# All sixteen gates ahead of the branches, and head pairs multiplied q first, then k, in a hybrid decoder step on one core

## The chip, the cores and the metric

The kernel runs on one core of one Trainium2 chip, in float32. The metric is the device time of one execution in microseconds (us); runs of a kernel on this one core agree within about 0.1%. Engines are named as in the profile: PE is TensorE (matrix products; PEld is its weight load), DVE is VectorE, ACT is ScalarE, POOL is GpSimd, SP is SyncE, which here issues most of the DMAs. SBUF is the on-chip memory, PSUM holds what TensorE writes.

## The reference

One layer (`DEPTH = 1`) of a hybrid decoder, for a prompt of 512 tokens and 8 single-token samples, 1024 wide. Both go through the same weights, so the kernel lays them side by side as 520 columns.

```
mod = silu(c) @ w_mod + b_mod                  # six parts: sh1, sc1, g1, sh2, sc2, g2
h   = rmsnorm(x) * (1 + sc1) + sh1
qa, fa, ia, oga, xb, yb, ga, gb = split(h @ w_in)      # eight parts of 1024
# branch A, HGRN2, 8 heads of 128: per token S = diag(f) S + k (x) v, o = S^T q
q = silu(qa); f = lb + (1 - lb) * sigmoid(fa); k = (1 - lb) * sigmoid(-fa)
o_a = rmsnorm(hgrn2(q, k, ia, log f)) * silu(oga)
# branch B, RG-LRU: causal conv of width 4, block-diagonal gates, a linear scan over time
o_b = rglru(conv(xb)) * gelu(yb)
merged = sigmoid(ga) * (o_a @ w_branch_a) + sigmoid(gb) * (o_b @ w_branch_b)
x = x + g1 * (merged @ w_out)
x = x + g2 * (relu(h2 @ w_ff1)^2 @ w_ff2),  h2 = rmsnorm(x) * (1 + sc2) + sh2
y = rmsnorm(x)
```

The final states of both recurrences are outputs too. The "gates" of this document are the two products with `ga` and `gb`, eight tiles of 128 rows each: sixteen in all. They depend on `h` alone; the products with `w_branch_a` and `w_branch_b` depend on the recurrences' results.

## The kernel before

**Products.** Everything is kept transposed, features on partitions, tokens along the row. A product (`gemm`, line 151 through `products`) makes 128 output rows for all 520 columns: 8 blocks of the sum, two column halves of 260, and three matmuls for each, because each float32 operand is split in a high and a low part that TensorE takes fast (`hi*hi + hi*lo + lo*hi`), 48 matmuls in all. It writes one of two PSUM tiles `mm`. A weight tile of 512 KB is loaded by SP into one of four slots `wst` (lines 101 and 103), rounded by ScalarE to `whi` (line 112) and subtracted by VectorE to `wlo` (line 115). `weights` sorts all tiles of the program in a fixed order: a tile is split two products ahead (`AHEAD`) and loaded three entries ahead (`LOADS`). Rows of w_mod (`ROWS`) go through the same slots and are used from there unsplit.

**Stages.** `begin` makes the modulation and `h`. Then come eight heads (`head`), each with four products (f, q, output gate, v), and between them the RG-LRU tiles (`rg_x`, `rg_y`). After each odd head, `heads_prompt` does the recurrence of the last two heads for the prompt. Then come the eight b gates, the eight products with w_branch_b, and eight times an a gate and the product with w_branch_a (`merge`); then w_out, and the MLP, which fills the second half of the time. Sixteen `mod` steps (two row tiles of w_mod, 16 small matmuls, line 413) are strewn among gates and branches by fixed rules (`mod_step`); they accumulate in PSUM pool `ppt`, which has one buffer, `pt`, and which the heads use too.

**heads_prompt.** A chunk of 128 tokens is treated by doubling: at level b (1, 2, 4, ... 64) TensorE takes the products of k of each block with q of the block after it (lines 664, 669, 673), then VectorE multiplies the decay of a block into the second blocks' q and the first blocks' k (line 681), VectorE or ScalarE picks the level's entries out (lines 688 and 691), and VectorE multiplies neighbouring decays into those of the next level (line 698). `X` holds, for each head, q times its decay (row 0), k (row 1) and q (row 2); four such tiles serve the eight heads in turn. `self.together()` raises the priority of what stands in it by 400.

**Order.** The program is a list of steps; a scheduler goes by priority (the program's order, unless raised) and its own estimate of readiness, and writes one fixed order for each engine. So an instruction may be ahead of an earlier step's, but at run time each engine keeps to that order.

**The hand-over.** After b gate number `TAIL` two steps stand: `end_recurrences` (the samples' norm, line 754 on) and `begin_tail`, which closes the pools of the heads, opens `misc`, `abb`, `tail` and `ab` in their memory and calls `load_branches`: 16 DMAs on POOL (lines 883 and 887) bring the recurrences' results back from DRAM, and ScalarE and VectorE split them (lines 205 and 206) to `a` (branch b's input) and `b` (branch a's). `reuse_waits="tile"` means that a tile in reused memory waits only for the old tiles it lies on. b gates use the eight slots `ma`, a gates two at a time the slots `t` of `tail`. The last work of a pair of heads is a row norm (lines 738 to 743), a transpose (747), the output multiplication (749), a store by SP (750), and for the samples line 632 and 634.

Of the kernel before, what the change touches and what calls it, by code (L numbers as in the profile page):

```python
# [6 lines left out]
F32 = mybir.dt.float32  # L7
# [4 lines left out]
OP = mybir.AluOpType  # L12
# [4 lines left out]
L = 512  # L17
NB = 8
T = L + NB
HALF = T // 2  # L20
KO = D // 128
# [3 lines left out]
DFF = 4 * D  # L25
EPS = 1e-6
AHEAD = 2
TAIL = 3
URGENT = 200
TOGETHER = 400  # L30
NWM = 8
# [45 lines left out]
class Kernel:  # L77
# [458 lines left out]
    def head_f(self, h, ps):  # L536

        nc = self.nc
        f = self.slot(self.ma, "ma")
        X = self.X[h % 4]  # L540
        k = X[:, 1]
        with self.urgent():
            self.sigmoid(self.two(f), ps)
            self.sigmoid(self.two(k), ps, scale=-1.0)
        nc.vector.tensor_scalar(f, f, self.lb1[:, h:h + 1], self.lbf[:, h:h + 1], OP.mult, OP.add)
        nc.vector.tensor_scalar(k, k, self.lb1[:, h:h + 1], None, OP.mult)
        return f, X

# [86 lines left out]

    def heads_prompt(self, hs):
        nc = self.nc
        two = [self.opened[h] for h in hs]
        tbs = [x[0][:, :L] for x in two]
        Xs = [x[1] for x in two]  # L640
        Ts = [self.hg.tile([128, 508], F32, name="tb", bufs=2) for _ in hs]
        to = 0
        a32 = self.hg.tile([128, 2, NC, 32], F32, name="a32", bufs=1)
        at = self.at

        def view(t, first_q, first_k, step, n, b):

            return bass.AP(tensor=t.tensor, offset=t.offset + first_q,
                           ap=[t.ap[0], [T + first_k - first_q, 2], [step, n], [1, b]])

        heads = lambda m, *shape: m[:, None].to_broadcast([128, 2, *shape])
        b = 1
        while b < C:
            n = L // (2 * b)
            p = self.pps.tile([128, 512], F32, name="ps")
            with self.together():
                for e, X in enumerate(Xs):
                    Q, K = X[:, 0], X[:, 1]
                    for c in range(NC):
                        if b == 1:  # L660
                            for j in range(4):
                                s, o = c * C + 32 * j, 256 * e + 64 * c
                                o = p[32 * j:32 * j + 32, o:o + 64].rearrange("p (x t) -> p x t", x=2)
                                nc.tensor.matmul(o, K[:, s:s + 32], X[:, 0::2, s:s + 32], start=True, stop=True)
                        elif b <= 32:
                            for j in range(0, 128, 32 if b < 32 else 64):
                                s, o = c * C + j, 128 * e + 32 * c
                                d = s if b < 32 else s + 32
                                nc.tensor.matmul(p[j:j + 32, o:o + 32], K[:, s:s + 32], Q[:, d:d + 32], start=True,
                                                 stop=True)  # L670
                        else:
                            s, o = c * C, 256 * e + 64 * c
                            nc.tensor.matmul(p[:64, o:o + 64], K[:, s:s + 64], Q[:, s + 64:s + 128], start=True,
                                             stop=True)
                if b == 64:
                    po = self.heads_sample(hs)
            for X, tb in zip(Xs, tbs):
                half = view(X, b, 0, 2 * b, n, b)
                fac = bass.AP(tensor=tb.tensor, offset=tb.offset, ap=[tb.ap[0], [1, 2], [2, n], [0, b]])
                with self.together():  # L680
                    nc.vector.tensor_tensor(half, half, fac, OP.mult)  # L681
            if b == 1:
                first = p.rearrange("p (e c x t) -> p e c x t", e=2, c=NC, x=2)
                nc.vector.tensor_tensor(a32, first[:, :, :, 1], heads(self.mdiag, NC, 32), OP.mult)
                p = first[:, :, :, 0]
            if b <= 16:
                p = p if b == 1 else p[:, :256].rearrange("p (e c t) -> p e c t", e=2, c=NC)
                nc.vector.copy_predicated(a32, heads(self.masks[b], NC, 32), p)
            elif b == 32:
                for j in (0, 64):  # L690
                    nc.scalar.copy(at[j:j + 32, :, :, j + 32:j + 64],
                                   p[j:j + 32, :256].rearrange("p (e c t) -> p e c t", e=2, c=NC))
            else:
                nc.scalar.copy(at[:64, :, :, 64:], p[:64].rearrange("p (e c t) -> p e c t", e=2, c=NC))
            for e, tb in enumerate(tbs):
                t2 = tb.rearrange("p (n two) -> p n two", two=2)
                tbs[e] = Ts[e][:, to:to + n]
                nc.vector.tensor_tensor(tbs[e], t2[:, :, 0], t2[:, :, 1], OP.mult)
            to += n
            b *= 2  # L700
        for j in range(0, 128, 32):
            nc.vector.tensor_copy(at[j:j + 32, :, :, j:j + 32], a32[j:j + 32])
        for e, h in enumerate(hs):
            self.head_prompt(h, tbs[e], at[:, e])
        self.heads_sample_done(hs, po)

    def head_prompt(self, h, tb, at):
# [847 lines left out]
    def run(self):  # L1555
# [24 lines left out]
        one = lambda name, m, fn, *a: steps.append(([(i[name][0], 0, m * 128)], fn, *a))  # L1580
        mods = [(p, k) for p in (2, 4, 3, 5) for k in range(0, KO, 2)]

        def mod_step():
            p, k = mods.pop(0)
            steps.append(([self.mod_key(p, k + n) for n in range(2)], self.mod, p, k))

        ga, gb = {}, {}
        self.rg = {}

        for h in range(H):  # L1590
            kf, kq, kv, kg = self.head_cols(h)
            steps.append(([kf, kq, kg, kv][FIRSTS if h == 0 else 0:], self.head_start if h == 0 else self.head, h))
            for n in (h - 1, h) if h % 2 else (h, h + 1):
                one("w_in", (40 if h % 2 else 32) + n, self.rg_y if h % 2 else self.rg_x, n)
        for m in range(KO):
            one("w_in", 56 + m, lambda m: gb.update({m: self.gate(7, m, self.slot(self.ma, "ma"))}), m)
            if m == TAIL:
                steps.append(([], self.end_recurrences))
                steps.append(([], self.begin_tail))
            if m > TAIL and m % 2:  # L1600
                mod_step()
        for m in range(KO):
            if m == 2:
                steps.append(([], self.rg_out))
            one("w_branch_b", m, lambda m: self.branch("w_branch_b", m, self.ob, gb[m]), m)
            if m <= TAIL or m % 2:
                mod_step()
        for m in range(KO):
            one("w_in", 48 + m, lambda m: ga.update({m: self.gate(6, m, self.slot(self.tail, "t"))}), m)
            one("w_branch_a", m, lambda m: self.merge(m, ga.pop(m), gb.pop(m)), m)  # L1610
            mod_step()
        steps.append(([], self.load_xT))
        steps.append(([], self.shifts))
        steps.append(([], self.begin_strassen))
# [20 lines left out]
    def begin(self):  # L1635
# [3 lines left out]
        nc = self.nc = InOrder(self.tc)  # L1639
# [69 lines left out]
        fs = self.start.tile([128, KO, NB], F32, name="fs")  # L1709
# [92 lines left out]
        nc = plain  # L1802
        self.rgp = self.open_pool("rg", 2, reuse_waits="tile")
        self.hg = self.scope.enter_context(self.tc.tile_pool(name="hg", bufs=2, reuse_waits="tile"))
        self.opened = {}
        self.X = [self.hg.tile([128, 3, T], F32, name=f"X{n}", bufs=1) for n in range(4)]
        self.fkq = [self.hg.tile([128, 3, 32], F32, name=f"fkq{n}", bufs=1) for n in range(4)]
        self.at = self.hg.tile([128, 2, NC, C], F32, name="at", bufs=1)
        for t in (*self.fkq, self.at):
# [19 lines left out]
    def begin_tail(self):  # L1829
        self.close_pool()  # L1830
        tc = self.tc
        pool = lambda name, bufs, **kw: tc.tile_pool(name=name, bufs=bufs, reuse_waits="tile", **kw)
        self.misc = self.ctx.enter_context(pool("misc", 1, side="right"))
        self.right = ExitStack()
        self.abb = self.right.enter_context(pool("abb", 16, side="right"))
        self.tail = self.open_pool("tail", 2, reuse_waits="tile")
        self.ab = self.scope.enter_context(pool("ab", 16))
        self.load_branches()

    def begin_strassen(self):  # L1840
        self.right.close()
        self.sw = self.ctx.enter_context(self.tc.tile_pool(name="sw", bufs=2, side="right", reuse_waits="tile"))


# [32 lines left out]
```

## Time and profile before

| | us |
|---|---|
| median of 3 runs (1031.09 to 1032.07) | 1031.99 |
| the profiled execution | 1030.22 |
| span of its trace, first to last instruction | 1028.4 |
| DVE busy (66% of the span) | 678.3 |
| ACT busy (50%) | 513.9 |
| POOL busy (12%) | 123.8 |

The granted TensorE clock is 0.995 on average. In the page, 40 slices of the span show where engines are busy (digits are tenths) and the DMA traffic:

```profile
DVE  7785868687586858355233347677776776777685
ACT  4555644644564554342122235466556655656663
DMA  9663353444334445268555568322672484274242
```

Slices are 25.7 us long. Heads take the third to the sixteenth slice, gates and branches the sixteenth to the twenty-fourth, w_out and the MLP the rest. Rows of groups read: line, engine, operation, output<-inputs, shapes, count, then busy time, mean ns of one, and the idle time of the engine before them with what ended it. Rows of the timeline read: start, length, engine, line, operation, count, and in brackets the idle time before.

### The profile page before, as it was taken

The page shows a single profiled execution, that of the slowest core. Times are in us where ns is not written, and L with a number is a line of the kernel's source. Part 1 is how long each engine was busy: PE and PEld are TensorE (multiplying, and loading weights), DVE is VectorE, ACT ScalarE, POOL GpSimd, SP SyncE. Part 2 cuts the span into 40 slices and gives each one's busy share as a digit, 9 for nine tenths or more (in the row PEclk, how much of TensorE's full clock was granted, in tenths as well). Part 3 has the DMA queues.
Part 4 walks back from the last instruction along what each step waited for, and adds up shares of the span by engine and source line. Part 5 has one row for each costly group of instructions (what it writes and reads, how often), then busy time and mean ns, then how long its engine had stood idle before and what let it go on. Part 6 is the DMA issues. An engine that isn't in the chain of part 4 may idle for free. (4 is left out here: it accounts for less than half of the span.)

```text
span 1028.4 us, 23561 instructions
## 1 busy us (share of the span) xinstructions
PE 997.9 (97%) x9756; PEld 965.4 (94%) x9756; DVE 678.3 (66%) x1428; ACT 513.9 (50%) x964; POOL 123.8 (12%) x229
## 2 busy tenths in 40 slices
PE   5999999999999999989999999999999999999997
PEld 2899899999999999969999999999999999999997
DVE  7785868687586858355233347677776776777685
ACT  4555644644564554342122235466556655656663
POOL 3210000000000001011000001011421231232150
PEclk9999999999999999999999999999999999999998
DMA  9663353444334445268555568322672484274242
GB/s 324 222 201 111 95 160 101 133 134 134 101 103 149 116 124 156 89 230 264 167 157 173 162 179 240 97 83 62 134 180 78 93 177 121 52 157 101 63 83 83
DMA packets 201822, 143.67 MB, mean 140 GB/s; under 512 B 6767, under 2 KB 189703, under 8 KB 201707
## 3 DMA queue, kind: packets, MB, share of 16 engines
q1 hardware_dynamic: 191090, 128.08, 41.5%
q0 software_dynamic: 10608, 14.05, 7.1%
q8 instruction: 76, 1.25, 0.5%
q14 instruction: 32, 0.25, 0.1%
q10 hardware_dynamic: 16, 0.03, 0.0%
HBM read 123.61 MB, written 11.26 MB: 131 GB/s over the span
## 5 line engine op out<-in xcount | busy, mean ns | idle before, releaser
L151 PE MATMUL mm<-h,whi 128*128 128x260 f32 (+1 forms) x2944 | 489.2, 285 | 0.0
L151 PEld LDWEIGHTS mm<-h,whi 128*128 128x128 f32 x2944 | 409.1, 188 | 4.5 <-ACT whi L112 3.3
L151 PE MATMUL mm<-h,wlo 128*128 128x260 f32 x1472 | 302.0, 284 | 0.0
L115 DVE TENSOR_TENSOR wlo<-wst,whi 128x1024 fp32r<-128x1024 f32 x164 | 200.1, 1221 | 124.8 <-ACT whi L112 123.2
L112 ACT CAST whi<-wst 128x1024 fp32r<-128x1024 f32 x164 | 171.8, 1049 | 214.5 <-PE mm L151 180.5
L151 PEld LDWEIGHTS mm<-h,wlo 128*128 128x128 f32 x1472 | 230.0, 189 | 0.4 <-issue 0.2
L151 PE MATMUL mm<-a,whi 128*128 128x260 f32 x512 | 84.3, 285 | 0.0
L151 PEld LDWEIGHTS mm<-a,whi 128*128 128x128 f32 x512 | 70.4, 188 | 2.5 <-issue 2.1
L151 PE MATMUL mm<-a,wlo 128*128 128x260 f32 x256 | 52.3, 284 | 0.0
L883 POOL DMA_DIRECT2D t<-obT_d x8 | 4.4, 552 | 386.8 <-PE pb L788 311.5
L1276 DVE TENSOR_TENSOR f<-f 128x260 f32<-128x260 f32 x64 | 27.3, 427 | 27.6 <-ACT f L1271 26.9
L1265 ACT ACTIVATE ft<-ft,fsh 128x512 f32<-128x512 f32 (+2 forms) x36 | 24.0, 675 | 36.1 <-DVE ft L1262 36.1
L151 PE MATMUL mm<-b,whi 128*128 128x260 f32 x256 | 41.1, 282 | 0.0
L1268 POOL TENSOR_TENSOR ft<-ft,fsh 128x8 f32<-128x8 f32 x28 | 18.5, 659 | 186.7 <-DVE ft L1262 146.5
L151 PEld LDWEIGHTS mm<-a,wlo 128*128 128x128 f32 x256 | 39.6, 188 | 0.0
L151 PEld LDWEIGHTS mm<-b,whi 128*128 128x128 f32 x256 | 35.0, 188 | 0.0
L1310 POOL DMA_DIRECT2D ma<-snap x28 | 27.7, 1002 | 35.0 <-issue 26.2
L681 DVE TENSOR_TENSOR X<-X,tb 128x512 f32<-128x512 f32 x48 | 31.8, 682 | 0.0
L1292 POOL DMA_DIRECT2D ma<-snap x28 | 25.9, 927 | 41.1 <-DMA ma<-snap 29.3
L1271 ACT ACTIVATE f<-ft 128x520 f32<-128x520 f32 (+1 forms) x36 | 20.8, 587 | 15.1 <-POOL ft L1269 13.0
L597 DVE SCALAR_TENSOR_TENSOR st<-vb,fkq,st 128x128 f32<-128x128 f32 x64 | 17.5, 345 | 14.6 <-DMA vb<-vd 14.6
L151 PE MATMUL mm<-b,wlo 128*128 128x260 f32 x128 | 25.9, 284 | 0.0
(571 smaller groups left out, 1871.3 us busy)
## 6 DMA issues: line engine op xcount, KB each, us to landing
wst<-in_w_in_dram SPq DMA_DIRECT2D x64, 512.0 KB, 4.2
wst<-in_w_mod_dram SPq DMA_DIRECT2D x32, 512.0 KB, 4.6
wst<-in_w_ff_dram SPq DMA_DIRECT2D x64, 256.0 KB, 3.6
wst<-in_w_ff_dram SPq DMA_DIRECT2D x32, 512.0 KB, 4.9
wm<-in_w_mod_dram SPq DMA_DIRECT2D x16, 512.0 KB, 10.5
st<-in_state_hgrn_dram SPq DMA_DIRECT2D x8, 512.0 KB, 5.2
vb<-vd SPq DMA_DIRECT2D x8, 512.0 KB, 3.4
out_dram<-st SPq DMA_DIRECT2D x8, 512.0 KB
```

The costliest lines, as they stand in the source:

```text
L112: ins = self.nc.scalar.copy(hi, st)
L115: self.nc.vector.tensor_tensor(lo, st, hi.bitcast(F32), OP.subtract)
L151: self.last_product = self.nc.tensor.matmul(ps[s][:, :c.stop - c.start], x, y[:, c], start=first and n == 0, stop=last and n == 2)
L597: nc.vector.scalar_tensor_tensor(st[:, b], vb[:, b], fkq[:, 1, b:b + 1], st[:, b], OP.mult, OP.add)
L681: nc.vector.tensor_tensor(half, half, fac, OP.mult)
L883: nc.gpsimd.dma_start(t, self.obT_d[n])
L1265: nc.scalar.activation(t[:, :p], t[:, :p], AF.Relu, bias=sh[:, 0:1])
L1268: eng.tensor_tensor(t[:, p:], t[:, p:], sh[:, 1:9], OP.add)
L1271: nc.scalar.activation(f, self.two(self.ft)[:, a:a + n], AF.Square)
L1276: self.nc.vector.tensor_tensor(f[:, n], f[:, a], f[:, b], op)
L1292: nc.gpsimd.dma_start(x[1][:, b], v[:, :n], accum_op=OP.add)
L1310: nc.gpsimd.dma_start(x[t][:, a], s[p], accum_op=OP.add)
```

## The change

`TAIL` goes from 3 to 6: the two hand-over steps stand behind the seventh b gate instead of the fourth. All sixteen gates stand ahead of all branch products: b0 to b7, a0 to a7, then the eight w_branch_b and the eight w_branch_a products. The a gates get a pool of their own, `gp`, with eight slots on the right side of SBUF, where `misc` was; `misc` is opened in `begin_strassen` instead. The `mod` steps are spread evenly over the 25 steps behind b6.

In `heads_prompt` the two heads of a pair share one tile `X` ([128, 2, 3, T]; two such tiles, the first in a pool of its own, `hx`) and one tile of decays. A level's multiplications take q of both heads in one instruction and then k of both, where one instruction took q and k of one head; level 1, whose decays lie in two tiles, has four instructions of half the size. The next decays are made for both heads at once.

```diff
-TAIL = 3
+TAIL = 6
...
-        X = self.X[h % 4]
+        X = self.X[h // 2 % 2][:, h % 2]
...
-        Ts = [self.hg.tile([128, 508], F32, name="tb", bufs=2) for _ in hs]
+        X = self.X[hs[0] // 2 % 2]
+        T_ = self.hg.tile([128, 2, 508], F32, name="tb", bufs=1)
+        fs = [self.opened[h][0] for h in hs]
...
+        def halves(x, b, n):
+
+            return X[:, :, x, :L].rearrange("p e (n two b) -> p e n two b", two=2, b=b)[:, :, :, 1 - x]
+
+        def factors(t, x, b):
+            return t.rearrange("p e (n two) -> p e n two", two=2)[:, :, :, x, None].to_broadcast([128, 2, L // (2 * b), b])
...
-            for X, tb in zip(Xs, tbs):
-                half = view(X, b, 0, 2 * b, n, b)
-                fac = bass.AP(tensor=tb.tensor, offset=tb.offset, ap=[tb.ap[0], [1, 2], [2, n], [0, b]])
-                with self.together():
-                    nc.vector.tensor_tensor(half, half, fac, OP.mult)
+            with self.together():
+                for x in range(2):
+                    half = halves(x, b, n)
+                    if b > 1:
+                        nc.vector.tensor_tensor(half, half, factors(tbs, x, b), OP.mult)
+                    else:
+                        for e, f in enumerate(fs):
+                            t2 = f[:, :L].rearrange("p (n two) -> p n two", two=2)
+                            nc.vector.tensor_tensor(half[:, e, :, 0], half[:, e, :, 0], t2[:, :, x], OP.mult)
...
-            for e, tb in enumerate(tbs):
-                t2 = tb.rearrange("p (n two) -> p n two", two=2)
-                tbs[e] = Ts[e][:, to:to + n]
-                nc.vector.tensor_tensor(tbs[e], t2[:, :, 0], t2[:, :, 1], OP.mult)
+            tn = T_[:, :, to:to + n]
+            if b > 1:
+                t2 = tbs.rearrange("p e (n two) -> p e n two", two=2)
+                nc.vector.tensor_tensor(tn, t2[:, :, :, 0], t2[:, :, :, 1], OP.mult)
+            else:
+                for e, f in enumerate(fs):
+                    t2 = f[:, :L].rearrange("p (n two) -> p n two", two=2)
+                    nc.vector.tensor_tensor(tn[:, e], t2[:, :, 0], t2[:, :, 1], OP.mult)
+            tbs = tn
...
-        def mod_step():
+        def mod_step(due):
+            if due < 0.999 or not mods:
+                return due
             p, k = mods.pop(0)
             steps.append(([self.mod_key(p, k + n) for n in range(2)], self.mod, p, k))
+            return due - 1
...
-        for m in range(KO):
-            one("w_in", 56 + m, lambda m: gb.update({m: self.gate(7, m, self.slot(self.ma, "ma"))}), m)
-            if m == TAIL:
+        tiles = [("b", m) for m in range(KO)] + [("a", m) for m in range(KO)]
+        share, due = len(mods) / (2 * len(tiles) - TAIL - 1), 0.0
+        for g, m in tiles:
+            if g == "b":
+                one("w_in", 56 + m, lambda m: gb.update({m: self.gate(7, m, self.slot(self.ma, "ma"))}), m)
+            else:
+                one("w_in", 48 + m, lambda m: ga.update({m: self.gate(6, m, self.slot(self.gp, "gp"))}), m)
+            if (g, m) == ("b", TAIL):
                 steps.append(([], self.end_recurrences))
                 steps.append(([], self.begin_tail))
-            if m > TAIL and m % 2:
-                mod_step()
-        for m in range(KO):
-            if m == 2:
+            if (g, m) > ("b", TAIL) or g == "a":
+                due = mod_step(due + share)
+        for g, m in tiles:
+            if (g, m) == ("b", 2):
                 steps.append(([], self.rg_out))
-            one("w_branch_b", m, lambda m: self.branch("w_branch_b", m, self.ob, gb[m]), m)
-            if m <= TAIL or m % 2:
-                mod_step()
-        for m in range(KO):
-            one("w_in", 48 + m, lambda m: ga.update({m: self.gate(6, m, self.slot(self.tail, "t"))}), m)
-            one("w_branch_a", m, lambda m: self.merge(m, ga.pop(m), gb.pop(m)), m)
-            mod_step()
+            if g == "b":
+                one("w_branch_b", m, lambda m: self.branch("w_branch_b", m, self.ob, gb[m]), m)
+            else:
+                one("w_branch_a", m, lambda m: self.merge(m, ga.pop(m), gb.pop(m)), m)
+            due = mod_step(due + share)
...
-        self.X = [self.hg.tile([128, 3, T], F32, name=f"X{n}", bufs=1) for n in range(4)]
+        hx = self.scope.enter_context(self.tc.tile_pool(name="hx", bufs=1, reuse_waits="tile"))
+        self.X = [p.tile([128, 2, 3, T], F32, name=f"X{n}", bufs=1) for n, p in enumerate((hx, self.hg))]
...
-        self.misc = self.ctx.enter_context(pool("misc", 1, side="right"))
         self.right = ExitStack()
+        self.gp = self.right.enter_context(pool("gp", 8, side="right"))
...
     def begin_strassen(self):
         self.right.close()
+        self.misc = self.ctx.enter_context(self.tc.tile_pool(name="misc", bufs=1, side="right", reuse_waits="tile"))
```

More of the change, by code (lines that the diff above doesn't have):

```diff
@@ L637, in heads_prompt @@
         nc = self.nc
-        two = [self.opened[h] for h in hs]
-        tbs = [x[0][:, :L] for x in two]
-        Xs = [x[1] for x in two]
-        Ts = [self.hg.tile([128, 508], F32, name="tb", bufs=2) for _ in hs]
+        X = self.X[hs[0] // 2 % 2]
+        T_ = self.hg.tile([128, 2, 508], F32, name="tb", bufs=1)
+        fs = [self.opened[h][0] for h in hs]
         to = 0
@@ L644, in heads_prompt @@
         at = self.at
-        def view(t, first_q, first_k, step, n, b):
-            return bass.AP(tensor=t.tensor, offset=t.offset + first_q,
-                           ap=[t.ap[0], [T + first_k - first_q, 2], [step, n], [1, b]])
+        def halves(x, b, n):
+            return X[:, :, x, :L].rearrange("p e (n two b) -> p e n two b", two=2, b=b)[:, :, :, 1 - x]
+        def factors(t, x, b):
+            return t.rearrange("p e (n two) -> p e n two", two=2)[:, :, :, x, None].to_broadcast([128, 2, L // (2 * b), b])
         heads = lambda m, *shape: m[:, None].to_broadcast([128, 2, *shape])
@@ L656, in heads_prompt @@
             with self.together():
-                for e, X in enumerate(Xs):
-                    Q, K = X[:, 0], X[:, 1]
+                for e in range(2):
+                    Q, K = X[:, e, 0], X[:, e, 1]
                     for c in range(NC):
@@ L663, in heads_prompt @@
                                 o = p[32 * j:32 * j + 32, o:o + 64].rearrange("p (x t) -> p x t", x=2)
-                                nc.tensor.matmul(o, K[:, s:s + 32], X[:, 0::2, s:s + 32], start=True, stop=True)
+                                nc.tensor.matmul(o, K[:, s:s + 32], X[:, e, 0::2, s:s + 32], start=True, stop=True)
                         elif b <= 32:
@@ L703, in heads_prompt @@
         for e, h in enumerate(hs):
-            self.head_prompt(h, tbs[e], at[:, e])
+            self.head_prompt(h, tbs[:, e], at[:, e])
         self.heads_sample_done(hs, po)
@@ L1594, in run @@
                 one("w_in", (40 if h % 2 else 32) + n, self.rg_y if h % 2 else self.rg_x, n)
-        for m in range(KO):
-            one("w_in", 56 + m, lambda m: gb.update({m: self.gate(7, m, self.slot(self.ma, "ma"))}), m)
-            if m == TAIL:
+        tiles = [("b", m) for m in range(KO)] + [("a", m) for m in range(KO)]
[6 more added lines that the diff above has]
+            if (g, m) == ("b", TAIL):
                 steps.append(([], self.end_recurrences))
                 steps.append(([], self.begin_tail))
-            if m > TAIL and m % 2:
-                mod_step()
-        for m in range(KO):
-            if m == 2:
+            if (g, m) > ("b", TAIL) or g == "a":
+                due = mod_step(due + share)
+        for g, m in tiles:
+            if (g, m) == ("b", 2):
                 steps.append(([], self.rg_out))
-            one("w_branch_b", m, lambda m: self.branch("w_branch_b", m, self.ob, gb[m]), m)
-            if m <= TAIL or m % 2:
-                mod_step()
-        for m in range(KO):
-            one("w_in", 48 + m, lambda m: ga.update({m: self.gate(6, m, self.slot(self.tail, "t"))}), m)
-            one("w_branch_a", m, lambda m: self.merge(m, ga.pop(m), gb.pop(m)), m)
-            mod_step()
+            if g == "b":
[3 more added lines that the diff above has]
+            due = mod_step(due + share)
+        assert not mods, mods
         steps.append(([], self.load_xT))
```

## The prediction

> **What bounds the kernel now.** I read the page's busy sums first, then the windows by stage, then TensorE's timeline where a window is not full, and last the queues that feed that place.
>
> ```profile
> PE 997.9 (97%) x9756; PEld 965.4 (94%) x9756; DVE 678.3 (66%) x1428; ACT 513.9 (50%) x964; POOL 123.8 (12%) x229
> ```
>
> TensorE is the bound: 97% busy, the next engine 66%. The change neither removes nor adds a matrix product, so it can only win TensorE's empty or slowed time, and lose by making more of it. The windows say where that is:
>
> ```profile
> 60.00:400.00 340.00, 335.56 (x4104) 328.30 (x4103) 250.12 (x631) 187.24 (x384) 4.26 (x7) 1.00 0.44 130
> 400.00:441.70 41.70, 41.69 (x381) 41.07 (x379) 17.08 (x45) 13.28 (x34) 0.00 (x0) 1.00 0.30 94
> 441.70:461.00 19.30, 14.55 (x114) 9.83 (x114) 11.08 (x33) 8.07 (x16) 4.33 (x8) 0.91 0.71 244
> 461.00:612.00 151.00, 151.00 (x1344) 141.43 (x1343) 57.28 (x75) 39.46 (x52) 4.56 (x11) 1.00 0.59 182
> ```
>
> (The columns: window, its length, then busy time and count of PE, PEld, DVE, ACT, POOL, then granted clock, DMA share, GB/s). The heads (60 to 400) lose 340.00 - 335.56 = 4.4 us. From 400 to 441.70 and from 461 to 612 nothing is lost. Between, 441.70 to 461, lies the worst place: 4.75 us idle in 19.3, and a clock of 0.91. What TensorE does there:
>
> ```profile
> 441.29 0.40 PE L151 MATMUL mm<-h,wlo 128*128 128x260 f32 x2
> 443.42 0.66 PE L747 MATMUL pt<-ident,g 128*128 128x128 f32 x4 [1.73 <-ACT g L743]
> 444.86 0.65 PE L632 MATMUL pt<-ident,sev 128*128 128x128 f32 x4 [0.79 <-DVE e L749]
> 445.78 3.48 PE L413 MATMUL pt<-wst,cT 128*32 128x256 f32 x30 [0.27 <-DVE os L634]
> 449.18 0.43 PE L758 MATMUL ps<-sq,ones_r 128*128 128x64 f32 x2
> ...
> 450.10 0.39 PE L871 MATMUL ps<-ident,xlast 128*11 128x128 f32 x2
> ...
> 452.49 0.64 PE L151 MATMUL mm<-a,whi 128*128 128x260 f32 x4
> ...
> 453.20 0.64 PE L151 MATMUL mm<-a,whi 128*128 128x260 f32 x4
> ...
> 456.06 0.62 PE L413 MATMUL pt<-wst,cT 128*32 128x256 f32 x2 [1.98 <-DMA wst<-in_w_mod_dram]
> ...
> 466.24 1.07 PE L413 MATMUL pt<-wst,cT 128*32 128x256 f32 x16
> ```
>
> At 441.29 the last of the eight b gates ends (`mm<-h`). After it TensorE has only the dependent end of heads 6 and 7: it waits for ScalarE (1.73), VectorE (0.79) and the last copy L634 (0.27), runs two blocks of `mod` and starts on the branches (`mm<-a`), where it waits 1.98 us for rows of w_mod. The product loop's own pace is six matmuls in 453.20 - 452.49 = 0.71 to 0.73 us, so a full product of 48 is about 5.75 us; an undisturbed `mod` of 16 matmuls is 1.07 us.
>
> **Gates first: the gap filled.** The stretch from 441.70 to 460.40 is 18.7 us long. Work in it at undisturbed prices: two transposes of four, 0.66 + 0.65; three `mod`, 3 x 1.07; L758 0.43; L871 0.39; one product, 5.75. Sum 11.1 us, so 7.6 us are lost. Merged rows overlap by their tails, 0.1 to 0.2 us for each of the seven groups, so up to 8.4 us may be lost. I take 8.0. It divides into the four waits above (4.8), and slowness that three windows show:
>
> ```profile
> 445.78:450.20 4.42, 4.42 (x35) 1.90 (x36) 3.32 (x6) 2.85 (x6) 2.38 (x5) 0.64 0.59 183
> ...
> 454.00:456.06 2.06, 0.08 (x2) 0.00 (x1) 0.69 (x3) 0.62 (x1) 0.00 (x0) 1.00 1.03 406
> 456.06:460.40 4.34, 4.34 (x34) 2.83 (x35) 3.69 (x18) 1.88 (x3) 1.61 (x3) 1.00 1.08 359
> ```
>
> After the idle time the granted clock is 0.64 for 4.42 us, 4.42 x 0.36 = 1.6 us; after 456.06 TensorE does 16 matmuls of `mod` (1.07) and some 18 of the product (2.15) in 4.34 us, another 1.1.
>
> The new order puts eight a gates (`self.h` times w_in, which need nothing of the heads) between the b gates and the branches, with the `mod` blocks spread by `share` = 16 / (32 - 7) = 0.64 for each step after b6. Adding 0.64 from b7 on and issuing at 1 gives a `mod` behind a0, a2, a3, a5 and a6. So behind 441.70 TensorE has 8 x 5.75 + 5 x 1.07 = 51.4 us of work of its own before branch b0, to 493. What the branches wait for is over long before:
>
> ```profile
> 445.55 0.17 DVE L634 COPY os<-pt 128x16 f32<-128x16 f32 x1 [0.75 <-PE pt L632]
> ...
> 446.56 3.14 DVE L206 TENSOR_TENSOR a<-t,a 128x520 fp32r<-128x520 f32 x5 [0.84 <-ACT a L205]
> ...
> 458.17 0.70 DVE L206 TENSOR_TENSOR a<-t,a 128x520 fp32r<-128x520 f32 x1
> ```
>
> The heads end at 445.7, the eight splits of `ob` at 458.9: 34 us ahead of 493. If that cover were gone the 8.0 us come back. That the gates may run ahead of the heads' end is what the present trace does with b4 to b7: they stand behind `begin_tail` in the program and yet are done at 441.69. Their results go to eight new slots in pool `gp`; were those slots in memory that heads 6 and 7 still hold, the two `mm` banks would still take a0 and a1, 11.5 us, past 445.7, so this costs 0 either way.
>
> **The queues that the gates are moved past.** Each gate and branch loads 512 KB of weights on SP, each `mod` two rows of 512 KB; 16 loads of branch inputs go out on POOL, now behind b6 instead of b3.
>
> ```profile
> 436.49 0.33 SPq L101 DMA_DIRECT2D wst<-in_w_mod_dram  x1
> 444.83 0.33 SPq L750 DMA_DIRECT2D oaT_d<-e  x1
> 446.92 0.38 SPq L103 DMA_DIRECT2D wst<-in_w_branch_b_dram  x1
> ```
>
> Now the rows of the first two `mod` fill the four `wst` slots until L413 runs at 445.78 (its one `pt` bank belongs to the heads until L634), and SP stands 8 us at head 7's store L750; the first branch weights go out at 446.92 only. In the new order the first `mod` is behind a0, so before the heads end at most one pair of rows is held and two slots go on serving gates; weights for two products, 11.5 us, are split ahead. Behind L750 on SP then stand gate weights; that wait lasts to 444.83 and TensorE would be in a0. Cost 0; with the cover gone, up to the 2.0 us of the w_mod wait.
>
> ```profile
> wst<-in_w_branch_b_dram SPq DMA_DIRECT2D x6, 512.0 KB, 10.9
> t<-oaT_d POOLq DMA_DIRECT2D x8, 256.0 KB, 6.7
> t<-obT_d POOLq DMA_DIRECT2D x3, 260.0 KB, 8.0
> ```
>
> From 446 to 475 the new order moves these 11 loads (2.8 MB), five gate weights (2.6) and three `mod` (3.1): 8.5 MB, 24 us at the 359 GB/s of the last window row above. It fits in 29 us, tightly; landing took 10.9 us at 1.03 to 1.08 share, about the 11.5 us of lead. I take 0; bound 1.98 + 1.1 = 3.1 us, today's loss at that load. In the Trainium skill, "DMA: Bandwidth & Descriptors" (Issuing engines are not separate DMA queues), transfers begun by POOL and SP share the same engines and interleave: by that rule the loads on POOL do slow the gate weights, which would put this bound into the sum; the share of 1.03 agrees that one load fills them.
>
> **The heads: q of both, then k of both.**
>
> ```profile
> L669 PE MATMUL ps<-X 128*32 128x32 f32 x1152 | 15.8, 199 | 4.4 <-DVE X L681 4.1 <-DVE a L688 0.2
> L681 DVE TENSOR_TENSOR X<-X,tb 128x512 f32<-128x512 f32 x48 | 31.8, 682 | 0.0
> L681 DVE TENSOR_TENSOR X<-X,ma 128x512 f32<-128x512 f32 x8 | 5.2, 694 | 9.2 <-PE ps L664 9.2
> L698 DVE TENSOR_TENSOR tb<-ma 128x256 f32<-128x256 f32 x8 | 3.4, 424 | 0.2
> L698 DVE TENSOR_TENSOR tb<-tb 128x128 f32<-128x128 f32 x8 | 2.3, 293 | 0.2
> L698 DVE TENSOR_TENSOR tb<-tb 128x64 f32<-128x64 f32 x8 | 1.8, 223 | 0.2
> L698 DVE TENSOR_TENSOR tb<-tb 128x32 f32<-128x32 f32 x8 | 1.5, 190 | 0.2
> L698 DVE TENSOR_TENSOR tb<-tb 128x16 f32<-128x16 f32 x8 | 1.4, 173 | 0.2
> L698 DVE TENSOR_TENSOR tb<-tb 128x8 f32<-128x8 f32 x8 | 1.3, 165 | 0.2
> L698 DVE TENSOR_TENSOR tb<-tb 128x4 f32<-128x4 f32 x8 | 1.3, 162 | 0.3
> ```
>
> For each of four pairs of heads: levels 2 to 64 keep two multiplications of 512 elements (0.68). Level 1 gets four of 256 (nearest row 424) for two of 694: +0.31 us. The factor products of those six levels become one for both heads instead of two: old 2 x (293 + 223 + 190 + 173 + 165 + 162) = 2.41 us, new 424 + 293 + 223 + 190 + 173 + 165 = 1.47: -0.94. VectorE gains 0.63 us a pair, 2.5 in all, beside TensorE; on the path it counts 0. What TensorE loses in the heads are waits of L669 for L681, 4.1 us. One of them:
>
> ```profile
> 200.67 0.68 DVE L681 TENSOR_TENSOR X<-X,tb 128x512 f32<-128x512 f32 x1
> ...
> 201.61 1.21 DVE L115 TENSOR_TENSOR wlo<-wst,whi 128x1024 fp32r<-128x1024 f32 x1
> 202.74 0.68 DVE L681 TENSOR_TENSOR X<-X,tb 128x512 f32<-128x512 f32 x1
> ```
>
> Between the two heads' multiplications stood a weight split of 1.21 us; TensorE did one head's 32 small matmuls and waited for the other's. With the new order the first head's matmuls wait for the k multiplication too, but both heads' matmuls mostly run as one block today, so the block's start is set by the second multiplication before and after. Another order may cure all of it or double it: -4.4 to +4.4; I take 0. Moving X of heads 0, 1, 4, 5 to pool `hx` changes which old tile the first k waits for, some tenths at 60 us, and is left at 0.
>
> **The sum.** The profiled execution took 1030.22 us (span 1028.4), 1.77 under the median of the runs, 1031.99. 1030.22 - 8.0 = 1022.2; on the median's footing 1031.99 - 8.0 = 1024.0.
>
> **Rivals.** (1) DMA crowding: gate weights or w_mod rows come late while the branch loads run; 3.1 us are lost again: 1027.1. For it: 10.9 us to landing; against it: nothing is lost after 461 at 1.03 and more. (2) The gap only moves: the instruction order keeps the gates behind the heads' end, or a wait of the same size opens ahead of the branches; nothing won, 1032.0. Against it: b4 to b7 run ahead today. (3) The other side: the heads are coupled. From level 2 on TensorE's in-order stream cannot begin a head's matmuls until both multiplications are through. Wherever TensorE arrives before the second, it stands one pitch of VectorE longer, about 0.60 us (1.28 us for two back to back, less 0.68). Six levels in four pairs: 24 x 0.60 = 14.4 us, 1038.4; it outweighs the gates from 14 of 24 levels on. For it: L669 waits already; against it: 4.1 us in 28 levels, and levels come one product (5.75 us) apart, with other work in between. In the Trainium skill, "Perfetto Trace Analysis" (Optimizing Scalar/DVE Operations), breaking up instructions is advised where an unsaturated engine causes bubbles elsewhere, which speaks against joining heads; VectorE's 66% fits its condition.
>
> **How the numbers follow.** The forecast, 1024.0, has 0.57, with its own range of 1019.2 (all 4.4 of the heads and the 8.4) to 1028.4 (heads doubled). DMA crowding 0.15, the gap moved 0.09, the heads coupled 0.12; 0.07 is for a gain by a cause I did not see or a mishap elsewhere. The 8-in-10 range is 1019.2 to 1031. About 0.2%, 2 us, is what a measurement tells from no change. Faster: 0.57 + 0.15 + about 0.05 = 0.77; same: 0.09 and 0.01 = 0.10; slower 0.13.
>
> **What would show it.** Right: between the last b gate and the first branch TensorE shows no wait over 1 us, the clock stays at 1.00, `mm<-h` runs to about 490, and the total of idle before L747, L632 and L413 falls from 4.8 to under 1. Crowding would show as waits of L151 or L413 on `wst` between 445 and 475. Coupling would show in L669's idle: over 8 us. Wrong altogether, if idle of the size of 441 to 456 stands ahead of the first `mm<-a`.

## The result and the profile after

| | us |
|---|---|
| before, median of 4 runs on the same chip | 1031.54 (1029.10 to 1032.07) |
| changed kernel, median of 4 runs | 1021.66 (1019.80 to 1023.16) |
| ratio, 95% interval | 0.9908 (0.9883 to 0.9933) |
| profiled executions, before and after | 1030.22 and 1022.73 |

The change makes the kernel 9.9 us faster by the medians, 6.9 to 12.1 by the interval, and 7.5 us in the two profiled executions; a gain of 8.0 and a time of 1024.0 were forecast. Runs of one kernel spread more than the 0.1% stated at the top: the four runs before span 0.3%. First the page's line of busy sums of the changed kernel, then its windows by stage, cut at the same times as before (window, length, PE, PEld, DVE, ACT, POOL, clock, DMA share, GB/s):

```profile
PE 996.0 (98%) x9756; PEld 966.2 (95%) x9756; DVE 673.5 (66%) x1412; ACT 514.0 (50%) x964; POOL 123.9 (12%) x229
```

```profile
60.00:400.00 340.00, 336.77 (x4113) 330.08 (x4112) 247.01 (x614) 186.33 (x381) 4.25 (x7) 0.99 0.44 131
400.00:441.70 41.70, 41.70 (x381) 41.30 (x382) 15.08 (x32) 14.44 (x30) 0.00 (x0) 1.00 0.28 84
441.70:461.00 19.30, 19.30 (x175) 17.55 (x174) 9.42 (x28) 8.99 (x24) 2.72 (x5) 1.00 0.47 139
461.00:612.00 151.00, 150.15 (x1340) 139.18 (x1341) 64.82 (x102) 41.48 (x56) 7.66 (x15) 1.00 0.70 211
```

PE has as many matmuls as before. In the window of the old gap it is now busy for all 19.30 us, with 175 matmuls instead of 114, at a clock of 1.00. PE's timeline of the changed kernel, of the product rows only the last of a gate (`mm<-h`) and the first of a branch (`mm<-a`) (L757 was L747, L768 was L758):

```profile
450.60 0.60 PE L757 MATMUL pt<-ident,g 128*128 128x128 f32 x4
454.28 0.60 PE L632 MATMUL pt<-ident,sev 128*128 128x128 f32 x4
457.47 0.64 PE L413 MATMUL pt<-wst,cT 128*32 128x256 f32 x8
...
467.69 0.64 PE L413 MATMUL pt<-wst,cT 128*32 128x256 f32 x8 [0.76 <-DMA wst<-in_w_mod_dram]
...
494.88 0.41 PE L151 MATMUL mm<-h,wlo 128*128 128x260 f32 x2
495.12 0.64 PE L151 MATMUL mm<-a,whi 128*128 128x260 f32 x4
```

The dependent end of the heads (L757 and L632) is still there, and no row of it has idle time before it: gates run between its pieces, and the last gate ends at 495. It is 9 us later (L632 at 454.28, formerly 444.86), which costs nothing: TensorE has work all the while. One wait for a row of w_mod is left.

In the heads 340.00 - 336.77 = 3.2 us are idle, formerly 4.4. But they lie closer together, and the clock fell behind them. Groups of PE, by line, then a window behind the largest wait:

```profile
L670 PE MATMUL ps<-X 128*32 128x32 f32 x1152 | 15.6, 199 | 2.0 <-DVE X L686 2.0
L632 PE MATMUL pt<-ident,sev 128*128 128x128 f32 x16 | 2.9, 313 | 1.2 <-DVE e L759 1.2
```

```profile
376.00:380.00 4.00, 3.99 (x21) 3.60 (x22) 4.00 (x8) 2.59 (x4) 0.00 (x0) 0.58 0.56 173
```

4.00 x 0.42 = 1.7 us of clock are lost here, so the heads lose 4.9 us where they lost 4.4.

### The profile page after: what moved, and what is told of

Read it like the earlier page. It is cut to its first block, busy times and chain, and to the rows that moved or that the text cites. A ratio compares the mean times of both kernels' runs of the same rounds, so it can differ in the third digit from the quotient of the medians.

```text
span 1020.9 us, 23540 instructions
## 1 busy us (share of the span) xinstructions
PE 996.0 (98%) x9756; PEld 966.2 (95%) x9756; DVE 673.5 (66%) x1412; ACT 514.0 (50%) x964; POOL 123.9 (12%) x229
## 5 line engine op out<-in xcount | busy, mean ns | idle before, releaser
L175 ACT ACTIVATE gate<-pb,pa 128x260 f32<-128x260 f32 x32 | 15.4, 482 | 21.0 <-PE pb L798 21.0
```

Of the source, the lines that this page charges most:

```text
L175: ins = self.nc.scalar.activation(out, x, AF.Sigmoid, **kw)
```

## The experiments

Three theories had to be told apart: the gates fill the gap (A); the joined multiplications carry part of the gain (B); and, after the third run, that the place of the first `mod` steps decides (D). Rival C in the texts below is that of the coupled heads. Each run was timed beside the kernel before on the same chip, whose median there was 1030.41 to 1031.42 us; small differences are therefore read from the ratios.

### The two halves of the change, each alone

`heads_prompt`, `X` and the decays as before, everything else changed (shown against the changed kernel):

```diff
-        X = self.X[h // 2 % 2][:, h % 2]
+        X = self.X[h % 4]
...
-                for x in range(2):
-                    half = halves(x, b, n)
+            for X, tb in zip(Xs, tbs):
+                half = view(X, b, 0, 2 * b, n, b)
```

> All gates first, TAIL 6 and the even spread of mod, but heads_prompt, X and the decays as before. Theory A (the gates fill the gap of 441 to 460 us and the heads count nothing): about 8 us under the kernel before, 1023.5 us, within 2 us of the changed kernel; idle of PE before the first branch product under 1.5 us. Rival B (the joined multiplications carry a good part of the 9.9 us): 4 to 6 us under the kernel before, 1025.5 to 1027.5.

Measured: 1023.07 us, ratio 0.9918 (0.9905 to 0.9931).

And the reverse, the kernel before with the changed `heads_prompt`, `X` and decays:

> The joined multiplications, shared X and decays alone; gates, TAIL and mod as before. Theory A: no change, 1031.5 us within 2 us; the gap of about 8 us at the end of the heads is still there. Rival B: 4 to 6 us faster, 1025.5 to 1027.5. Rival C (the heads are coupled and the gates hide it): slower by 4 us or more, 1035.5, with over 8 us of idle before L669's matmuls (its line in this kernel).

Measured: 1031.12 us, ratio 0.9999 (0.9990 to 1.0009). The 4 to 6 us of B are not there, and A stands: the new order of gates, hand-over and `mod` carries all that is clear of the noise. PE's timeline of this second kernel at the end of the heads shows that the gap is still there:

```profile
440.31 0.39 PE L743 MATMUL pt<-g,X 128*128 128x128 f32 x2
445.55 1.12 PE L757 MATMUL pt<-ident,g 128*128 128x128 f32 x4 [4.86 <-ACT g L753]
447.46 1.11 PE L632 MATMUL pt<-ident,sev 128*128 128x128 f32 x4 [0.79 <-DVE e L759]
448.84 3.63 PE L413 MATMUL pt<-wst,cT 128*32 128x256 f32 x30 [0.27 <-DVE os L634]
```

But the gap takes in what may have been won ahead of it, so this run does not show that the joined multiplications change nothing. TensorE reaches the gap 1 us earlier, at 440.7 instead of 441.7. The last products of the heads (L743) now stand behind the last b gate, where they stood ahead of it (L733 at 437.93), and the wait before the transpose is 4.86 us instead of 1.73. With the gap filled, the joined multiplications can be worth the difference between 0.9918 and 0.9908, about 1 us, which the intervals do not tell from nothing.

### How many gates the gap needs

Two of the a gates (`AF`; in a second kernel four) ahead of the branch products, the others each ahead of its own w_branch_a product; `mod` still spread evenly:

```diff
-        for g, m in tiles:
...
+        AF = 2
...
+        for m in range(AF):
+            gate_a(m)
+            due = mod_step(due + share)
+        for m in range(KO):
...
+        for m in range(KO):
+            if m >= AF:
+                gate_a(m)
+                due = mod_step(due + share)
```

> Only two of the a gates ahead of the branch products, six again each ahead of its own w_branch_a product; all else as in the changed kernel. Theory A: the cover ends at 441.7 + 2 x 5.75 + two mod 2.1 = 455 us, while the eighth split of the branch input ended at 458.9 in the kernel before; about 3.5 us are lost again, 1025 us, as a wait ahead of the first branch product. Rival (any work past the heads' end at 445.7 is enough): no loss, 1021.7 us. Rival (the splits only start later when more is ahead of them): loss of 6 us or more.

> Four a gates ahead of the branch products instead of two or eight. Theory A: cover to 441.7 + 4 x 5.75 + 2 or 3 mod = 467.5 us, past the last split at 458.9 of the kernel before; no loss against the changed kernel, 1021.7 us within 2. Rival (in the changed kernel the last split ended at 469.7, because work put ahead delays it, and the loads still crowd): 2 to 4 us slower than the changed kernel, 1024 to 1026.

Measured: with two 1025.76 us, ratio 0.9941 (0.9926 to 0.9956); with four 1021.83, ratio 0.9916 (0.9898 to 0.9935), as with all eight. The size of the loss with two, 4.1 us against the changed kernel by the medians and 3.4 by the ratios, is what was expected (3.5); its place is not, so the agreement in size is luck. PE's timeline with two gates ahead (rows of `mod` alone):

```profile
455.44 1.50 PE L413 MATMUL pt<-wst,cT 128*32 128x256 f32 x24 [0.27 <-DVE os L634]
...
466.73 0.64 PE L413 MATMUL pt<-wst,cT 128*32 128x256 f32 x8 [0.27 <-DMA wst<-in_w_mod_dram]
469.51 0.63 PE L413 MATMUL pt<-wst,cT 128*32 128x256 f32 x6 [2.15 <-DMA wst<-in_w_mod_dram]
...
477.27 0.64 PE L413 MATMUL pt<-wst,cT 128*32 128x256 f32 x8 [0.94 <-DMA wst<-in_w_mod_dram]
```

Ahead of the first branch product, at 457.50, there is a wait of 0.27 us only; 3.4 us of waits for w_mod rows lie among the first branch products, while the 11 branch loads run. With four or eight gates ahead these waits are 0.2 and 0.8 us. More gates in front give the loads time.

### The hand-over and the first mod steps

The changed kernel with one number changed:

```diff
-TAIL = 6
+TAIL = 3
```

> The changed kernel with TAIL 3 instead of 6: the hand-over steps again behind the fourth b gate; all gates still first. Theory A (what fills the gap is the eight a gates, not where the hand-over stands): within 2 us of the changed kernel, 1021.7 us. Rival (with the hand-over early, the first mod is due behind b5, its rows hold the weight slots until the heads end, and weights come late): 3 us or more slower than the changed kernel, 1025 or over, with waits of PE for w_in or w_mod loads between 440 and 470 us.

Measured: 1030.08 us, ratio 0.9997 (0.9985 to 1.0010). All gates are still ahead of the branches, and the whole gain is gone. The profiled execution of this kernel was the longest of its 12 (1034.66 us). PE's timeline, the rows with idle time before them:

```profile
449.56 0.66 PE L757 MATMUL pt<-ident,g 128*128 128x128 f32 x4 [1.73 <-ACT g L753]
451.01 1.08 PE L632 MATMUL pt<-ident,sev 128*128 128x128 f32 x4 [0.78 <-DVE e L759]
452.36 2.96 PE L413 MATMUL pt<-wst,cT 128*32 128x256 f32 x32 [0.27 <-DVE os L634]
...
458.98 0.75 PE L151 MATMUL mm<-h,whi 128*128 128x260 f32 x4 [1.48 <-ACT whi L112]
462.43 1.23 PE L151 MATMUL mm<-h,whi 128*128 128x260 f32 x4 [2.27 <-ACT whi L112]
```

The waits of the gap are those of the kernel before, and after it gates (`mm<-h`) wait for their weights to be split. They had been loaded late. SP's timeline, first of this kernel, then of the changed one:

```profile
400.27 6.91 SPq L101 DMA_DIRECT2D wst<-in_w_mod_dram  x2
...
424.95 0.38 SPq L103 DMA_DIRECT2D wst<-in_w_in_dram  x1
429.32 0.33 SPq L101 DMA_DIRECT2D wst<-in_w_mod_dram  x1
431.25 0.33 SPq L760 DMA_DIRECT2D oaT_d<-e  x1
435.56 0.33 SPq L101 DMA_DIRECT2D wst<-in_w_mod_dram  x1
440.22 0.34 SPq L736 DMA_DIRECT2D out_dram<-g  x1
450.98 0.33 SPq L760 DMA_DIRECT2D oaT_d<-e  x1
453.50 1.24 SPq L103 DMA_DIRECT2D wst<-in_w_in_dram  x2
```

```profile
422.95 4.70 SPq L101 DMA_DIRECT2D wst<-in_w_mod_dram  x2
429.26 0.33 SPq L760 DMA_DIRECT2D oaT_d<-e  x1
433.57 0.38 SPq L103 DMA_DIRECT2D wst<-in_w_in_dram  x1
438.23 0.34 SPq L736 DMA_DIRECT2D out_dram<-g  x1
440.67 0.38 SPq L103 DMA_DIRECT2D wst<-in_w_in_dram  x1
447.98 0.33 SPq L101 DMA_DIRECT2D wst<-in_w_mod_dram  x1
451.95 0.33 SPq L760 DMA_DIRECT2D oaT_d<-e  x1
```

With `TAIL` 3 the even spread begins three steps earlier, so two `mod` stand behind b5 and b7. Their four rows of w_mod go out at 400.27 (two), 429.32 and 435.56. After 424.95 no gate weights go out until 453.50, 1.1 us after `mod` has begun (452.36). SP itself stands at head 7's store (L760) until 450.98, so for most of that time the store holds SP, and the slots, full until `mod` has run, hold it last. The changed kernel has one pair of w_mod rows in the slots up to 447.98 and loads gate weights at 433.57 and 440.67, ahead of that store. That suggests theory D: four rows of w_mod, which `mod` cannot use until the heads give back `pt`, hold the four `wst` slots. But `TAIL` also moves the hand-over. Two kernels separate the two: the hand-over behind b3 with `mod` spread as in the changed kernel, and the hand-over behind b6 with two early `mod`:

```diff
-            if (g, m) == ("b", TAIL):
+            if (g, m) == ("b", 3):
```

> The hand-over steps behind the fourth b gate as in the run with TAIL 3, but the mod steps spread as in the changed kernel, the first behind gate a0. Theory D (in the run with TAIL 3 the w_mod rows of two early mod steps held all four weight slots until the heads ended, so the a gates had no weights): the gain is back, 1021.7 us within 2 us, and PE runs gates through 450 to 460 us. Rival (the place of the hand-over itself, by its priority, moves the end of the heads or the loads): 1028 us or more.

```diff
-        share, due = len(mods) / (2 * len(tiles) - TAIL - 1), 0.0
+        share, due = (len(mods) - 2) / (2 * len(tiles) - KO), 0.001
...
+            if (g, m) in (("b", 5), ("b", 7)):
+                mod_step(1)
-            if (g, m) > ("b", TAIL) or g == "a":
+            if g == "a":
                 due = mod_step(due + share)
```

> The changed kernel, hand-over behind b6, all gates first, but with the first two mod steps behind b5 and b7 as in the kernel before; the other 14 spread evenly. Theory D (rows of w_mod in the weight slots until the heads end starve the a gates): the gain is gone, 1029 to 1031.5, PE idle by more than 4 us between 441 and 465 although gates are ready. Rival (the hand-over's place is what counts): 1021.7.

And the kernel before with no `mod` among the b gates and one behind each branch product:

```diff
-            if m > TAIL and m % 2:
-                mod_step()
...
-            if m <= TAIL or m % 2:
-                mod_step()
+            mod_step()
```

> The kernel before with one edit: no mod among the b gates, one behind each branch product instead; gates, heads and hand-over as before. Theory (before the change two things bound the gap: no independent work and no free weight slots; without gates ahead the branches still wait for the heads' end at 445.7 and the splits up to 458.9): 0 to 3 us faster than before, 1028.5 to 1031.5. Rival (the held slots alone made the gap): 8 us faster, 1023.5.

Measured, as ratios to the kernel before:

| order of the gates | mod behind b5 and b7 | first mod later |
|---|---|---|
| a gates with the branches | 1 (the kernel before) | 0.9985 (0.9972 to 0.9997), 1029.23 us |
| all first, hand-over behind b3 | 0.9997 (0.9985 to 1.0010), 1030.08 us | 0.9917 (0.9897 to 0.9937), 1022.03 us |
| all first, hand-over behind b6 | 1.0011 (0.9996 to 1.0026), 1030.11 us | 0.9908 (0.9883 to 0.9933), 1021.66 us |

The place of the hand-over makes no difference in either column. Gates first alone: nothing. Late `mod` alone: 0.15%, some 2 us, with an interval that nearly reaches zero. Both: 0.8 to 0.9%. D stands as far as the place of the first `mod` decides. That it does so through the slots rests on SP's rows above and the waits for `whi`; no run changed the number of slots. The window from 441.70 on in the kernel with the hand-over behind b6 and early `mod`:

```profile
441.70:470.00 28.30, 22.75 (x166) 17.21 (x165) 16.77 (x51) 11.79 (x22) 5.41 (x10) 0.82 0.70 231
```

5.5 us idle and a clock of 0.82 over 28 us, with a gates ready but for their weights.

### The wait left in the heads

VectorE's timeline of the changed kernel, ahead of PE's largest waits:

```profile
370.79 1.93 DVE L597 SCALAR_TENSOR_TENSOR st<-vb,fkq,st 128x128 f32<-128x128 f32 x7 [3.75 <-DMA vb<-vd]
372.63 0.76 DVE L686 TENSOR_TENSOR X<-X,ma 128x256 f32<-128x256 f32 x2
373.30 0.35 DVE L597 SCALAR_TENSOR_TENSOR st<-vb,fkq,st 128x128 f32<-128x128 f32 x1
373.57 0.76 DVE L686 TENSOR_TENSOR X<-X,ma 128x256 f32<-128x256 f32 x2
```

The update of the samples' state (L597) waits 3.75 us for a DMA, and the level 1 multiplications (L686), for which PE waits, stand behind it. In the kernel before, at the same place, the level 1 multiplications (L681) stood ahead of the update:

```profile
373.43 1.31 DVE L681 TENSOR_TENSOR X<-X,ma 128x512 f32<-128x512 f32 x2 [3.08 <-PE ps L664]
377.22 2.19 DVE L597 SCALAR_TENSOR_TENSOR st<-vb,fkq,st 128x128 f32<-128x128 f32 x8 [2.49 <-DMA vb<-vd]
```

So the joined multiplications traded one loss for another. In the run of that half alone TensorE has no idle time from 60 to 366 and from 384 to 400 us, where the kernel before has 4.1 us; but from 366 to 384 it idles 2.8 us (0.4 before), at a clock of 0.81 over these 18 us (1.00 before).

The update was put in a function, called for odd heads behind level 2:

```diff
+        def update():
+            for b in range(NB):
+                nc.scalar.activation(st[:, b], st[:, b], AF.Copy, scale=fkq[:, 0, b:b + 1])
+                nc.vector.scalar_tensor_tensor(st[:, b], vb[:, b], fkq[:, 1, b:b + 1], st[:, b], OP.mult, OP.add)
...
         while b < C:
+            if b == 4:
+                self.update()
```

> The changed kernel with the sample state update of each odd head (lines 596 and 597, which wait for a DMA on VectorE's in-order stream ahead of level 1) moved behind level 2 of the pair's recurrence. Theory: the waits of PE at 372 to 378 us (2.4 us idle in the last pair) and the throttled 4 us behind them (1.7 us) go; 3 to 4 us faster than the changed kernel, 1018 us. Rival (level 1 is late for another reason, or the update blocks as much at its new place): no change, 1021.7.

Measured: 1021.51 us, ratio 0.9912 (0.9894 to 0.9930): no change. The scheduler had put the update back ahead of level 1, presumably because its estimate has the DMA landed earlier:

```profile
370.33 1.93 DVE L599 SCALAR_TENSOR_TENSOR st<-vb,fkq,st 128x128 f32<-128x128 f32 x7 [3.88 <-DMA vb<-vd]
372.18 0.75 DVE L695 TENSOR_TENSOR X<-X,ma 128x256 f32<-128x256 f32 x2
```

So the order was forced (`level1` is the last multiplication of level 1):

```diff
+                if first:
+                    self.behind(ins, first)
...
+                self.update(level1)
```

> As the run that deferred the odd heads' state update, but with an order forced on VectorE: the update's instructions stand behind the pair's level 1 multiplications (the deferral alone was undone by the scheduler, which takes the update as ready before its DMA lands). Theory: level 1 no longer waits for the DMA; PE's waits at 373 to 376 us (2.4 us) and the slow clock that may follow go; 2 to 4 us faster than the changed kernel, 1018 to 1019.5. Rival (another instruction, or the next wait, takes their place): within 1 us of the changed kernel, 1021.7.

Measured: 1018.05 us (1017.85 to 1019.27), ratio 0.9887 (0.9871 to 0.9904). That is 3.6 us under the changed kernel by the medians and 2.2 by the ratios, whose intervals overlap (0.9883 to 0.9933 there). Against the gates alone (0.9918, 0.9905 to 0.9931) the intervals are apart: the joined multiplications together with this order are worth some 3 us. VectorE's timeline and the heads' window:

```profile
368.11 1.44 DVE L697 TENSOR_TENSOR X<-X,ma 128x256 f32<-128x256 f32 x4 [1.26 <-PE ps L676]
...
370.94 2.19 DVE L599 SCALAR_TENSOR_TENSOR st<-vb,fkq,st 128x128 f32<-128x128 f32 x8 [1.06 <-DMA vb<-vd]
```

```profile
60.00:400.00 340.00, 340.00 (x4152) 333.60 (x4151) 249.42 (x618) 188.46 (x384) 4.23 (x7) 1.00 0.44 132
```

The multiplications start at 368.11 instead of 372.63, and the wait for the DMA shrinks to 1.06 us; PE is busy for all 340 us of the heads.

## Why the prediction was right, point by point

**The gap of 8.0 us.** The size holds: the order of the gates without the heads' part won 8.35 us (1031.42 - 1023.07), and the window 441.70 to 461 has nothing idle. The first product with w_out starts at 603.20 instead of 611.36, 8.2 us earlier. The two windows 441.70 to 612 lost 4.75 us of idle time and 1.7 us of clock before, 0.85 us after; that is 5.6 us, and what makes up the rest, such as the slow matmuls priced at 1.1, no run took apart. One line of the sum is off: seven groups at 0.1 to 0.2 us are 0.7 to 1.4, so up to 9.0 us and not 8.4 might have been lost. The 8.0 does not hang on it; the lower end of the range, 1019.2, would be 1018.6.

**Why the gap was there.** This step was incomplete. The prediction put the gap down to a lack of independent work and had the held slots as a side remark, priced at 0, or 2.0 us with the cover gone. The table shows two necessary conditions: independent work, and a later first `mod`, which by SP's rows means free slots to bring that work's weights. Gates first with four rows of w_mod loaded early win nothing, so what was priced at 0 to 2.0 us is worth all 8 to 9. The forecast came out right because the change does both; the note that the first `mod` then stands behind a0, which leaves two slots to the gates, turned out to be its main point, not a condition that costs nothing.

**Cover.** 51.4 us of gates and `mod` were counted against an end of the splits at 458.9. The heads' end came 9 us later than before, since its pieces now queue among gates, and the last split of `ob` ended at 469.8; the first branch product came at 495.12, so 25 of the 34 us of cover were left. The signs named for a right forecast are there: no wait over 0.76 us between the last b gate and the first branch, a clock of 1.00, gates to 495, and idle time before L747, L632 and L413 down from 4.8 to 0.8 us. The run with two gates cost 3.4 to 4.1 us, that with four nothing.

**The queues.** Taken at 0 with a bound of 3.1; measured 0.8 us of waits for w_mod in the changed kernel, 3.4 with two gates ahead. The share of 1.03 that the prediction read from 454 to 456 us was that of several loads under way, so it does not show that one load fills the DMA engines; a row of w_mod alone (issued at 429.44 in the kernel before) does so for under 1 us, with a share of 1.04 from 431.25 to 431.50. In the Trainium skill, "DMA: Bandwidth & Descriptors" (Issuing engines are not separate DMA queues), loads of POOL and SP share the engines; by the direction the run with two gates agrees, but the changed kernel shows that where the lead is long enough it costs under 1 us.

**The heads, taken at 0.** The run of that half alone gives 0.9999 (0.9990 to 1.0009), but the 0 is a balance and in part luck. The prediction held that the second multiplication sets the start of a block before and after; in fact L669's waits went wherever they stood (4.1 us), and new ones of 2.8 us, with a slowed clock, came around level 1 of the last pair (1.6 at L670, 1.2 at L632), where the update now stood ahead of level 1. In the changed kernel idle time in the heads fell by 1.2 us and slow clock took 1.7. The rival of coupled heads is excluded: it asked for over 8 us of idle time at L669, and the run of that half alone has 1.6 (L670 there). With it falls, for this change, the reason against it that the prediction took from the Trainium skill, "Perfetto Trace Analysis" (Optimizing Scalar/DVE Operations), breaking up instructions where an unsaturated engine causes bubbles: what made PE wait was an unrelated instruction ahead of the multiplications, not that two heads share one.

**VectorE.** 2.5 us less were counted; its busy time fell by 4.8 (678.3 to 673.5), off the path.

## What to carry to other kernels

Work moved into a gap fills it only if its operands can arrive: look at what holds the load buffers while the consumer is stalled, and do not let entries whose consumer waits behind the stall take buffers that independent work needs. An instruction that waits for a DMA on an in-order engine charges its wait to all behind it; a scheduler with an optimistic landing time will put it first, and moving it in the program may not be enough without a forced order. A change beside the bound engine can remove its waits at one place and make new ones at another: a sum of nothing does not mean that nothing changed, so compare the waits place by place.

## What was not expected of the hardware

The same idle time may or may not slow the clock. In the changed kernel PE's waits of 0.87, 0.39 and 1.18 us near 373 to 376 us were followed by a clock of 0.58 for 4 us. The kernel with the deferred update has waits of 1.01, 0.39 and 1.17 us at the same place, and the clock stayed at 1.00:

```profile
376.00:380.00 4.00, 4.00 (x34) 3.83 (x33) 4.00 (x8) 2.13 (x4) 0.00 (x0) 1.00 0.60 188
```

The Trainium skill, "TensorE: Matmul & The Clock Gate" (Part 1: The HAM clock gate), says that activity is judged in free-running windows that do not start with the kernel; that could explain it. The two traces do not speak against it, but no run here shows the windows. The spread of the runs goes with the clock in part: of the six runs of the deferred update, three have mean clocks of 0.996 to 0.997 and take 1020.08 to 1020.64 us, and three have 0.993 to 0.994 and take 1022.38 to 1022.84. The kernel without waits in the heads spreads over 1.4 us only; its mean clocks still go from 0.994 to 0.999, so the waits in the heads are not all that moves the clock.
